# Second layer's tile of four experts: one expert's chunk to a ring tile, in rows of 4 KB instead of 2 KB

## The chip, the cores and the metric

The kernel runs on one core of one Trainium2 chip. The metric is the device time of one launch in microseconds (us); times of runs are given as the median of three.

## The reference

Two layers, each a mixer (three kinds of attention) and then a mixture of 16 experts. Only the experts of the second layer bear on this change. There the tokens are the 256 of the latent sequence, each routed to two experts:

```
def moe(tokens, router_w, router_b, w1, w3, w2):      # w1, w3: 16 x 1024 x 512; w2: 16 x 512 x 1024, f32
    ...
    gates = jnp.sum(jax.nn.one_hot(eidx, N_EXPERTS) * wsel[..., None], 1)
    def expert_step(acc, p):
        w1e, w3e, w2e, ge = p
        y = (jax.nn.silu(tokens @ w1e) * (tokens @ w3e)) @ w2e
        return acc + ge[:, None] * y, None
    out, _ = lax.scan(expert_step, jnp.zeros_like(tokens), (w1, w3, w2, gates.T))
```

The weights of one expert are three matrices of 2 MB, 6 MB in all, and each expert's are read once.

## The kernel before

**Expert weights.** The host lays out `wexp[layer, expert, chunk]` as six chunks of 1 MB for each expert, each of 128 rows (partitions) by 2048 f32 (8 KB a row). Chunks 0 and 1 are w1, 2 and 3 are w3, 4 and 5 are w2. A chunk of w1 or w3 holds four slices of the contraction (`kk`), 512 columns each; a chunk of w2 holds two slices of 1024 columns.

**Tiles of tokens.** The experts are ranked by their number of tokens, and `PLANS[1]` packs them on tiles of 128 token rows: seven tiles, `t` = 0 to 6. Tile 1 has four experts with 32 rows each (`_four(8, 9, 10, 11)`), the six others two experts each. For a tile TensorE runs `up(t)` (four chunks: w1, then w3, out to PSUM), `hidden(t)` (four transposes), `down(t)` (the two chunks of w2), and around these `dispatch` (gathers the tile's tokens, line 1828), `to_tokens` (lines 1635, 1619) and `combine` (lines 1850, 1851). In the trace the matmuls of `up` are line 1672 and those of `down` line 1771; each f32 matmul of the program is two instructions there. The order on TensorE is the code's: up(0), dispatch(1), hidden(0), down(0), up(1) with the combines of tile 0 between its chunks 2 and 3, dispatch(2), up(2) with hidden(1) after its first chunk, dispatch(3), down(1), up(3), dispatch(4), down(2), and so on.

**The stream of weights.** All weights of the kernel go through one list (`want`) in the order in which they are used, and are loaded by DMAs issued on SyncE's queue (line 194 for a load of several pieces, 198 for one). The buffers are ring tiles of 1 MB, 16 of them in this stage. `ws.take()` hands the next loaded ring tile to TensorE's code; `ws.done()` gives its buffer back, and the next load of the list is written for that buffer. A load into a buffer waits until the matmuls that read the tile before it are done. Each DMA on the queue also waits for the eighth DMA ahead of it to land, since eight completion semaphores (DMAHW0 to DMAHW7) are used in turn: at most eight are in flight. The ring tiles are numbered through the program; the names w194 to w277 below are the last 84. In the list, in this order:

- w182 to w193: the 12 MB of tile 0;
- w194 to w209: chunks 0 to 3 of tile 1 (four experts, 16 MB);
- w210 to w217: chunks 0 to 3 of tile 2 (two experts, 8 MB);
- w218 to w225: chunks 4 and 5 of tile 1 (8 MB);
- w226 to w277: tile 3's chunks 0 to 3, tile 2's chunks 4 and 5, and so on, all of two experts.

The numbers of the experts from w194 on are read from a register that the router sets (line 1485).

**How a ring tile is filled.** With two experts a ring tile holds one half (1024 columns) of each one's chunk: two DMAs of 512 KB, rows of 4 KB. With four experts it holds a quarter (512 columns) of each one's chunk: four DMAs of 256 KB, rows of 2 KB. One `ws.take()` of the four-expert tile therefore serves one slice `kk` in `up` (four groups of 32 rows, one for each expert) or half a slice in `down`, and is followed by its `ws.done()`.

Of the kernel before, what the change touches and what calls it, by code (L numbers as in the profile page):

```python
# [132 lines left out]
class Stream:  # L133
# [29 lines left out]
    def pump(self, most=None, after=None):  # L163

        end = min(len(self.aps), self.known) if most is None else min(len(self.aps), self.known, self.next + most)
        while self.next < end:
            n = self.next
            for r in reversed(self.rings):
                if r["free"] and n < r["limit"]:
                    r["free"] -= 1  # L170
                    break
            else:
                r = None
                if not self.rooms:
                    return
            if r is None:
                t = self.rooms.pop(0)
                parts = [t[:, 0:1024], t[:, 1024:2048]]
            elif r["halves"]:
                parts = [r["pool"].tile([128, 1024], F32R, tag=t, name=f"w{n}")[:].bitcast(F32) for t in r["tag"]]  # L180
            else:
                t = r["pool"].tile([128, 2048], F32, tag=r["tag"], name=f"w{n}", bufs=r["bufs"])
                parts = [t[:, 0:1024], t[:, 1024:2048]]
            if after is not None:
                self.nc.scalar.copy(parts[0][:, 0:1], after)
            src = self.aps[n]
            if isinstance(src, tuple):
                if len(src) == 4:
                    parts = [p[:, 512 * k:512 * k + 512] for p in parts for k in range(2)]
                for p, s in zip(parts, src):  # L190
                    src = s() if callable(s) else s
                    if len(src.shape) == 3:
                        p = p.rearrange("p (k f) -> p k f", k=src.shape[1])
                    load = self.nc.sync.dma_start(p, src)
                self.tiles[n] = parts
            else:
                self.tiles[n] = t[:, :self.widths[n]]
                load = self.nc.sync.dma_start(self.tiles[n], src() if callable(src) else src)
            self.load_of[n] = load.ins
            self.ring_of[n] = r  # L200
            self.next += 1
# [35 lines left out]
def build(tc, x_in, ctx_in, wada, win, wout, wexp, wqkv, rw, prm_in, bro_in, lnr, cst_in, out, dbg=None):  # L237
# [4 lines left out]
    G, T, S = nc.gpsimd, nc.tensor, nc.sync  # L242
# [49 lines left out]
    def want_exp(l):  # L292
        def by_columns(s, c, n):
            w = weights(l, s, c)

            def half():
                src = w() if callable(w) else w
                return src.rearrange("p (k f) -> p k f", k=2)[:, :, 512 * n:512 * n + 512]
            return half

        def part(t, lo, hi):
            ss = slots_of(l, t)
            if l and (t, lo) == (len(PLANS[l]) - 1, 4):

                for n in range(2):
                    for c in range(lo, hi):
                        want(tuple(by_columns(s, c, n) for s in ss), 2048)
                return
            for c in range(lo, hi):
                if len(ss) == 1:  # L310
                    want(weights(l, ss[0], c), 2048)
                else:
                    w = 2048 // len(ss)
                    for k in range(len(ss)):
                        want(tuple(weights(l, s, c, slice(w * k, w * k + w)) for s in ss), 2048)

        n = len(PLANS[l])
        part(0, 0, 4)
        for t in range(n):
            if t + 1 < n:  # L320
                if l and t == 0:
                    part(0, 4, 6)
                if slots_of(l, t + 1)[0] == 2:
                    marks["known", l] = len(aps)
                if l and t + 2 == n:

                    part(t, 4, 6)
                part(t + 1, 0, 4)
            if l == 0 or (t and t + 2 != n):
                part(t, 4, 6)  # L330
# [872 lines left out]
    for l in range(DEPTH):  # L1203
# [443 lines left out]
        def up(t, between):  # L1647

            o = sbig()
            x = xs_of.pop(t)  # L1650
            for c in range(4):
                if len(plan[t]) == 1:
                    xH, xL = x
                    if not first_splits:
                        raw = ws.take()
                    ob = o[:, halves[c // 2]]
                    early = len(first_splits) > 0
                    for q in range(2):
                        h, lo = first_splits.pop(0) if early else wsplit(raw[:, 1024 * q:1024 * q + 1024])
                        kk = 4 * (c % 2) + 2 * q  # L1660
                        mm6([(ob, xH[:, kk + k, :], xL[:, kk + k, :], h[:, halves[k]], lo[:, halves[k]]) for k in range(2)],
                            kk == 0, kk == 6, (0, 2, 1))
                    if not early:
                        ws.done()
                else:
                    nq = 4 // len(plan[t])
                    for c2 in range(len(plan[t])):
                        raw = ws.take()
                        for q in range(nq):
                            kk = 4 * (c % 2) + nq * c2 + q  # L1670
                            for r0, r1, e in groups(t):
                                T.matmul(o[r0:r1, halves[c // 2]], lhsT=x[:, kk, r0:r1], rhs=raw[e][:, halves[q]],  # L1672
                                         start=(kk == 0), stop=(kk == 7), skip_group_check=True)
                        ws.done()
                for s in between[c]:
                    s()
            u = ex.tile([128, 512], F32, tag="u", name="u", bufs=2)
            A.activation(u, o[:, 0:512], AF.Sigmoid)
            V.scalar_tensor_tensor(u, u, gms.pop(t), o[:, 0:512], op0=ALU.mult, op1=ALU.mult)
            V.tensor_mul(u, u, o[:, 512:1024])  # L1680
            us[t] = u
# [17 lines left out]
        def down(t, between=((),) * 4, final=None, pieces=None):  # L1699
# [63 lines left out]
            else:  # L1763
                o = sbig()
                four = len(plan[t]) == 4
                for kk in range(4):
                    for n in range(2):
                        if four or n == 0:
                            raw = ws.take()
                        for r0, r1, e in groups(t):  # L1770
                            T.matmul(o[r0:r1, halves[n]], lhsT=u[:, kk, r0:r1], rhs=raw[e][:, halves[0 if four else n]],  # L1771
                                     start=(kk == 0), stop=(kk == 3), skip_group_check=True)
                        if four or n:
                            ws.done()
                    for s in between[kk]:
                        s()
            for n in range(2):
# [534 lines left out]
```

## Time and profile before

| | us |
|---|---|
| median of three runs | 1265.35 |
| lowest and highest | 1263.18, 1268.04 |
| the profiled execution | 1269.78 |
| its span, first to last instruction | 1268.0 |

The profiled execution is one run more; the difference of 1.78 between its time and its span lies around the program. Rows below are from its trace, with times in us from the start of the span.

### The profile page before, as it was taken

The page shows a single profiled execution, that of the slowest core. Times are in us where ns is not written, and L with a number is a line of the kernel's source. Part 1 is how long each engine was busy: PE and PEld are TensorE (multiplying, and loading weights), DVE is VectorE, ACT ScalarE, POOL GpSimd, SP SyncE. Part 2 cuts the span into 40 slices and gives each one's busy share as a digit, 9 for nine tenths or more (in the row PEclk, how much of TensorE's full clock was granted, in tenths as well). Part 3 has the DMA queues.
Part 4 walks back from the last instruction along what each step waited for, and adds up shares of the span by engine and source line. Part 5 has one row for each costly group of instructions (what it writes and reads, how often), then busy time and mean ns, then how long its engine had stood idle before and what let it go on. Part 6 is the DMA issues. An engine that isn't in the chain of part 4 may idle for free. (4 is left out here: it accounts for less than half of the span.)

```text
span 1268.0 us, 18050 instructions
## 1 busy us (share of the span) xinstructions
PE 1141.0 (90%) x6433; PEld 745.0 (59%) x6433; DVE 664.2 (52%) x1340; ACT 472.5 (37%) x871; POOL 349.4 (28%) x344
## 2 busy tenths in 40 slices
PE   6999999998996898999989689999989699899984
PEld 4898764556785655555466478975547443334431
DVE  3545375626568965654478666546545812012133
ACT  4423456335235544434145364545343210101112
POOL 0242220231043634543464356221140100101001
PEclk9999999998996899999989889999999799999996
DMA  9543008661446889999995212502675899999992
GB/s 351 177 141 131 1 1 308 262 262 67 176 161 239 312 326 374 394 400 412 414 350 234 84 43 87 187 11 99 216 278 204 308 351 371 343 410 408 409 403 102
DMA packets 79213, 310.75 MB, mean 245 GB/s; under 512 B 9344, under 2 KB 10512, under 8 KB 64784
## 3 DMA queue, kind: packets, MB, share of 16 engines
q1 hardware_dynamic: 70864, 287.77, 59.7%
q10 hardware_dynamic: 5376, 13.40, 3.0%
q0 software_dynamic: 2880, 8.39, 2.3%
q8 instruction: 52, 0.85, 0.3%
q14 instruction: 41, 0.34, 0.1%
HBM read 304.74 MB, written 6.89 MB: 246 GB/s over the span
## 5 line engine op out<-in xcount | busy, mean ns | idle before, releaser
L232 DVE TENSOR_TENSOR wl<-w,wh 128x640 fp32r<-128x640 f32 (+3 forms) x133 | 162.8, 1242 | 52.1 <-ACT wh L232 50.7
L232 ACT CAST wh<-w 128x1024 fp32r<-128x1024 f32 (+2 forms) x135 | 132.7, 1006 | 105.2 <-PE s L447 34.7
L1245 POOL TENSOR_TENSOR wl<-w,wh 128x384 fp32r<-128x384 f32 x96 | 129.1, 1384 | 121.9 <-ACT wh L232 119.7
L1672 PE MATMUL s<-w,x 128*32 128x512 f32 (+1 forms) x640 | 111.5, 609 | 5.3 <-DMA w<-in_wexp_dram 5.3
L1771 PE MATMUL s<-w,uH 128*32 128x512 f32 (+1 forms) x480 | 81.9, 596 | 1.6 <-DMA w<-in_wexp_dram 0.9
L232 DVE TENSOR_REDUCE mxv<-s 128x2 f32<-128x1024 f32 (+1 forms) x54 | 56.3, 1044 | 48.7 <-PE s L1113 20.1
L232 ACT ACTIVATE P<-s,mxv 128x512 f32<-128x512 f32 (+1 forms) x108 | 65.9, 618 | 41.3 <-DVE mxv L232 22.5
L1672 PEld LDWEIGHTS s<-w,x 128*32 128x32 f32 (+1 forms) x640 | 30.6, 121 | 72.1 <-issue 52.1
L232 DVE TENSOR_TENSOR yL<-s,yH 128x512 fp32r<-128x512 f32 x22 | 15.1, 687 | 81.9 <-ACT yH L232 81.8
L445 PE MATMUL acc<-wh,hH 128*128 128x384 f32 (+3 forms) x148 | 52.5, 358 | 4.3 <-ACT hH L232 4.3
L232 ACT ACTIVATE u<-s 128x512 f32<-128x512 f32 x19 | 11.3, 596 | 120.6 <-PE s L1672 112.3
L446 PE MATMUL s<-wl,hH 128*128 128x384 f32 (+2 forms) x148 | 52.8, 357 | 3.0 <-DVE wl L232 3.0
L1819 POOL TENSOR_TENSOR xr<-xr,lr 128x1024 f32<-128x1024 f32 x4 | 9.4, 2360 | 161.4 <-ACT lr L232 161.4
L1672 PE MATMUL s<-w,xH 128*32 128x512 f32 (+1 forms) x352 | 53.6, 595 | 0.0
L445 PE MATMUL s<-wh,hH 128*128 128x384 f32 (+2 forms) x148 | 52.9, 357 | 0.0
L447 PE MATMUL s<-wh,hL 128*128 128x384 f32 (+2 forms) x148 | 52.7, 356 | 0.0
L1771 PEld LDWEIGHTS s<-w,uH 128*32 128x32 f32 (+1 forms) x480 | 22.3, 118 | 51.1 <-issue 36.2
L446 PE MATMUL acc<-wl,hH 128*128 128x384 f32 (+3 forms) x148 | 51.7, 349 | 0.0
L1643 PE MATMUL s<-wl,xH 128*128 128x512 f32 x128 | 44.2, 422 | 7.5 <-DVE wl L232 6.9
L447 PE MATMUL acc<-wh,hL 128*128 128x384 f32 (+3 forms) x148 | 50.7, 352 | 0.0
L514 PE MATMUL acc<-w,sc 128*32 128x512 f32 x320 | 45.7, 602 | 3.9 <-DMA w<-in_wada_dram 3.9
L232 DVE SCALAR_TENSOR_TENSOR u<-u,gp,s 128x512 f32<-128x512 f32 x19 | 14.1, 742 | 65.8 <-ACT u L232 65.8
(534 smaller groups left out, 2531.3 us busy)
## 6 DMA issues: line engine op xcount, KB each, us to landing
w<-in_wexp_dram SPq DMA_DIRECT2D x236, 512.0 KB
w<-in_wexp_dram SPq DMA_DIRECT2D x48, 1024.0 KB
w<-in_wada_dram SPq DMA_DIRECT2D x46, 1024.0 KB
w<-in_wexp_dram SPq DMA_DIRECT2D x96, 256.0 KB
w<-in_win_dram SPq DMA_DIRECT2D x8, 1024.0 KB
w<-in_wout_dram SPq DMA_DIRECT2D x8, 1024.0 KB
w<-in_win_dram SPq DMA_DIRECT2D x9, 768.0 KB
row<-rowd ACTq DMA_DIRECT2D x9, 512.0 KB
```

The costliest lines, as they stand in the source:

```text
L232: return f(*args, **kw)
L445: T.matmul(o, lhsT=lh, rhs=rh, start=start, stop=False, skip_group_check=True)
L446: T.matmul(o, lhsT=lh, rhs=rl, start=False, stop=False, skip_group_check=True)
L447: T.matmul(o, lhsT=ll, rhs=rh, start=False, stop=stop, skip_group_check=True)
L514: T.matmul(box["o"][32 * c:32 * c + 32, :], lhsT=sc32[:, k, :], rhs=w[:, 512 * c:512 * c + 512], start=(k == 0), stop=(k == 7), skip_group ...
L1245: last_split[0] = G.tensor_tensor(lo[:, c:], raw[:, c:], h[:, c:].bitcast(F32), op=ALU.subtract).ins
L1643: T.matmul(o, lhsT=ll if ps_ == 2 else lh, rhs=rl if ps_ == 1 else rh, start=start and j == 0 and not (same and n), stop=stop and j == 2 a ...
L1672: T.matmul(o[r0:r1, halves[c // 2]], lhsT=x[:, kk, r0:r1], rhs=raw[e][:, halves[q]], start=(kk == 0), stop=(kk == 7), skip_group_check=True)
L1771: T.matmul(o[r0:r1, halves[n]], lhsT=u[:, kk, r0:r1], rhs=raw[e][:, halves[0 if four else n]], start=(kk == 0), stop=(kk == 3), skip_group ...
L1819: G.tensor_tensor(x1[:, i, :], x1[:, i, :], lr, op=op)
```

## The change

In the stream, the loads of the four-expert tile are no longer cut by columns across experts: for each chunk there are four ring tiles, one for each expert, each holding that expert's whole chunk as two halves of 1024 columns. The branch that cut ring tiles into four pieces goes. In `up`, TensorE's code takes four ring tiles at once, runs the four slices of the chunk with the expert's own tile as the right-hand side, and gives the four back after the last slice; `down` takes four, runs two slices, and gives the four back. The arithmetic, the order of the matmuls and the number of ring tiles stay.

```
             if isinstance(src, tuple):
-                if len(src) == 4:
-                    parts = [p[:, 512 * k:512 * k + 512] for p in parts for k in range(2)]
                 for p, s in zip(parts, src):
...
-                    w = 2048 // len(ss)
-                    for k in range(len(ss)):
-                        want(tuple(weights(l, s, c, slice(w * k, w * k + w)) for s in ss), 2048)
+                    cols = [slice(1024 * k, 1024 * k + 1024) for k in range(2)]
+                    if len(ss) == 4:
+
+                        for s in ss:
+                            want(tuple(weights(l, s, c, k) for k in cols), 2048)
+                        continue
+                    for k in cols:
+                        want(tuple(weights(l, s, c, k) for s in ss), 2048)
...
-                    nq = 4 // len(plan[t])
-                    for c2 in range(len(plan[t])):
-                        raw = ws.take()
-                        for q in range(nq):
-                            kk = 4 * (c % 2) + nq * c2 + q
+                    four = len(plan[t]) == 4
+                    for c2 in range(1 if four else 2):
+                        raw = [ws.take() for _ in range(4 if four else 1)]
+                        for q in range(4 if four else 2):
+                            kk = 4 * (c % 2) + 2 * c2 + q
                             for r0, r1, e in groups(t):
-                                T.matmul(o[r0:r1, halves[c // 2]], lhsT=x[:, kk, r0:r1], rhs=raw[e][:, halves[q]],
+                                rhs = raw[e][q // 2][:, halves[q % 2]] if four else raw[0][e][:, halves[q]]
+                                T.matmul(o[r0:r1, halves[c // 2]], lhsT=x[:, kk, r0:r1], rhs=rhs,
                                          start=(kk == 0), stop=(kk == 7), skip_group_check=True)
-                        ws.done()
+                        for n in range(ws.used - len(raw), ws.used):
+                            ws.done(n)
...
                 for kk in range(4):
+                    if not four or kk % 2 == 0:
+                        raw = [ws.take() for _ in range(4 if four else 1)]
                     for n in range(2):
-                        if four or n == 0:
-                            raw = ws.take()
                         for r0, r1, e in groups(t):
-                            T.matmul(o[r0:r1, halves[n]], lhsT=u[:, kk, r0:r1], rhs=raw[e][:, halves[0 if four else n]],
+                            rhs = (raw[e][kk % 2] if four else raw[0][e])[:, halves[n]]
+                            T.matmul(o[r0:r1, halves[n]], lhsT=u[:, kk, r0:r1], rhs=rhs,
                                      start=(kk == 0), stop=(kk == 3), skip_group_check=True)
-                        if four or n:
-                            ws.done()
+                    if not four or kk % 2:
+                        for n in range(ws.used - len(raw), ws.used):
+                            ws.done(n)
```

On SyncE's queue, the first loads of the four-expert tile, right behind the reading of the experts' numbers (a DMA's row names the ring tile and its shape in f32; what it waits for stands in brackets; the rows between that set its address are left out). Before, one ring tile:

```order
L194 DMA w194_8680<-in_wexp_dram 128x512 [waits DMAHW3_49]
...
L194 DMA w194_8680<-in_wexp_dram 128x512 [waits DMAHW4_49]
...
L194 DMA w194_8680<-in_wexp_dram 128x512 [waits DMAHW5_49]
...
L194 DMA w194_8680<-in_wexp_dram 128x512 [waits DMAHW6_49]
...
L194 DMA w195_8685<-in_wexp_dram 128x512 [waits DMAHW7_49]
```

And now two ring tiles, and the first that waits for a buffer:

```order
L192 DMA w194_8680<-in_wexp_dram 128x1024 [waits DMAHW3_49]
...
L192 DMA w194_8680<-in_wexp_dram 128x1024 [waits DMAHW4_49]
...
L192 DMA w195_8683<-in_wexp_dram 128x1024 [waits DMAHW5_49]
...
L192 DMA w195_8683<-in_wexp_dram 128x1024 [waits DMAHW6_49]
...
L192 DMA w198_8772<-in_wexp_dram 128x1024 [waits DMAHW3_49,PE_49]
```

A ring tile is two DMAs of twice the size, the tile's 96 DMAs become 48, and the eight in flight are 4 MB where they were 2 MB.

On TensorE, the start of `down(1)` (w218 and w219 are ring tiles, uH the hidden values; a row with x4 is one matmul for each of the four experts). Before:

```order
L1771 MATMUL s_9323<-w218_9057,uH_9204 32x512 x4
L1771 MATMUL s_9323<-w219_9066,uH_9204 32x512 x4
L1771 MATMUL s_9323<-w220_9075,uH_9204 32x512 x2
L1771 MATMUL s_9323<-w220_9076,uH_9204 32x512 x2
L1771 MATMUL s_9323<-w221_9085,uH_9204 32x512 x2
L1771 MATMUL s_9323<-w221_9086,uH_9204 32x512 x2
```

And now, where a row is one expert's matmul:

```order
L1777 MATMUL s_9275<-w218_9037,uH_9156 32x512
L1777 MATMUL s_9275<-w219_9040,uH_9156 32x512
L1777 MATMUL s_9275<-w220_9043,uH_9156 32x512
L1777 MATMUL s_9275<-w221_9047,uH_9156 32x512
...
L1777 MATMUL s_9275<-w222_9083,uH_9156 32x512
L1777 MATMUL s_9275<-w223_9087,uH_9156 32x512
```

The first matmuls read one ring tile before; now the first four read four of them, and none of the four is given back before the sixteenth.

## Rows read from the trace of the kernel before

**Rows 1.** The page: the span in 40 equal slices of 31.7 us.

```profile
DMA  9543008661446889999995212502675899999992
GB/s 351 177 141 131 1 1 308 262 262 67 176 161 239 312 326 374 394 400 412 414 350 234 84 43 87 187 11 99 216 278 204 308 351 371 343 410 408 409 403 102
```

**Rows 2.** The page: DMA issues, count and KB of each.

```profile
w<-in_wexp_dram SPq DMA_DIRECT2D x236, 512.0 KB
...
w<-in_wexp_dram SPq DMA_DIRECT2D x96, 256.0 KB
```

**Rows 3.** Windows: stretch, busy time of engines, granted clock, DMA share, GB/s.

```profile
1000.00:1009.00 9.00, 4.99 (x30) 5.02 (x31) 8.83 (x42) 0.59 (x1) 0.00 (x0) 0.59 0.70 236
1009.00:1060.00 51.00, 49.85 (x299) 20.05 (x299) 11.71 (x36) 5.35 (x10) 0.00 (x0) 1.00 1.01 341
1061.00:1080.00 19.00, 17.73 (x154) 7.66 (x154) 2.75 (x8) 2.71 (x5) 0.00 (x0) 1.00 1.03 410
1081.00:1106.00 25.00, 24.08 (x127) 9.41 (x128) 1.44 (x2) 2.97 (x5) 4.68 (x2) 1.00 0.99 331
1110.00:1230.00 120.00, 115.69 (x684) 48.24 (x678) 24.50 (x48) 15.03 (x27) 4.68 (x2) 0.99 1.03 408
...
1240.00:1250.00 10.00, 9.04 (x34) 2.56 (x30) 2.78 (x5) 0.62 (x1) 0.00 (x0) 0.86 0.18 71
```

**Rows 4.** Windows at the edges of these stretches, and from 1110 to 1115.

```profile
1060.00:1061.00 1.00, 1.00 (x3) 0.16 (x3) 0.00 (x0) 0.02 (x1) 0.00 (x0) 1.00 0.99 369
1080.00:1081.00 1.00, 0.34 (x7) 0.02 (x3) 0.00 (x0) 0.00 (x0) 0.00 (x0) 1.00 1.02 365
1107.00:1108.00 1.00, 0.00 (x1) 0.00 (x0) 0.28 (x1) 0.59 (x1) 0.00 (x0) 1.00 1.00 385
1110.00:1115.00 5.00, 5.00 (x36) 1.62 (x32) 0.00 (x0) 0.04 (x1) 0.00 (x0) 0.68 1.03 409
```

**Rows 5.** Waits of SyncE's queue, 960 to 1245: us in total, times, longest.

```profile
SPq L194 <- DMA w<-in_wexp_dram: 105.8, 158, 2.2
...
SPq L194 <- PE s L1672: 3.9, 11, 0.6
SPq L194 <- PE s L1771: 2.2, 8, 0.4
```

**Rows 6.** Timeline of TensorE around up(1): start, us, instructions, idle before.

```profile
1037.80 7.07 PE L1672 MATMUL s<-w,x 128*32 128x512 f32 x64
...
1045.52 3.64 PE L1672 MATMUL s<-w,x 128*32 128x512 f32 x32
...
1051.87 7.52 PE L1672 MATMUL s<-w,x 128*32 128x512 f32 x30
1059.90 1.04 PE L1672 MATMUL s<-w,x 128*32 128x512 f32 x2 [0.51 <-DMA w<-in_wexp_dram]
1060.87 3.84 PE L1828 MATMUL tp<-O,h2a 128*128 128x128 f32 x32
1064.64 1.92 PE L1672 MATMUL s<-w,x 128*32 128x512 f32 x16
```

**Rows 7.** Timeline of TensorE around down(1) and the start of up(3).

```profile
1088.58 6.85 PE L1771 MATMUL s<-w,uH 128*32 128x512 f32 x36
...
1099.90 7.11 PE L1771 MATMUL s<-w,uH 128*32 128x512 f32 x20 [0.16 <-DMA w<-in_wexp_dram]
1109.00 5.34 PE L1672 MATMUL s<-w,x 128*32 128x512 f32 x32 [1.99 <-DMA w<-in_wexp_dram]
```

**Rows 8.** Waits of TensorE's weight loads, 1037 to 1110.

```profile
PEld s L1771 <- DMA w<-in_wexp_dram: 12.4, 19, 1.5
PEld s L1672 <- DMA w<-in_wexp_dram: 12.1, 15, 1.6
```

**Rows 9.** Waits of TensorE's weight loads, 1110 to 1250.

```profile
PEld s L1672 <- DMA w<-in_wexp_dram: 6.8, 9, 1.5
...
PEld s L1771 <- DMA w<-in_wexp_dram: 0.3, 1, 0.3
```

## The prediction

> **What bounds the kernel now.** I read the page's slices first [rows 1]. The DMA digits say 9 in two late places; the last begins a little before slice 32 (32 x 31.7 = 1014 us) and holds until slice 38, so from the start of the second layer's experts the DMA engines are never idle. Busy is not fast, though: under the same 9s the line in GB/s says 351, 371, 343 and then 410. The page's list of DMAs shows what differs: 96 loads of 256 KB, the four-expert tile's and nothing else's, beside the 512 KB loads of the two-expert tiles [rows 2].
>
> The windows put the two side by side in the order of the stream [rows 3]. While w194 to w209 arrive (four experts, rows of 2 KB) the DMAs are busy 1.01 and move 341 GB/s; while w210 to w217 arrive (two experts, 4 KB) they move 410; w218 to w225 (four experts again) 331; everything behind, 408. The share of busy time is 0.99 to 1.03 in all four, so the engines are not kept waiting: they take longer for the same bytes. The windows at the edges [rows 4] read 369 at 1060, 365 at 1080 and 385 at 1107, each between the two levels, so the rate changes with the kind of load and not with what TensorE does.
>
> Is the stream what the end waits for? SyncE's queue waited 105.8 us in this stage for an older DMA to land (its eight in flight) and only 3.9 + 2.2 us for matmuls to free a buffer [rows 5]: the stream holds itself up, TensorE doesn't hold it. TensorE in turn waits for the stream, in `up(1)`, `up(2)`, `down(1)`: its weight loads waited 12.1 + 12.4 us for w from 1037 to 1110 [rows 8], and `up(3)` starts at 1109.00 on the landing of w226 [rows 7]. From 1110 on the waits are 6.8 + 0.3 us [rows 9], and the stream runs at 408 until it ends near 1242 (a share of 0.18 in the 10 us from 1240) [rows 3]: the two keep the same pace, and both start this last part from one event, the landing of w226 at 1109.0. What moves that event moves the end.
>
> **The change, part by part.**
>
> *The loads.* 96 DMAs of 256 KB become 48 of 512 KB: 16 + 8 ring tiles of 1.049 MB, 25.2 MB, the same bytes. Their form becomes that of the two-expert tiles' loads, 128 rows of 4 KB, which have their rate in the trace: 410 GB/s, so 2.557 us for a ring tile. Two ways to get the gain:
> - By landing times. By the windows' sum, w192 and w193, 2.1 MB, are all there is before w194: 9.0 us at 236 GB/s [rows 3] is 2.1 MB, so w194 begins near 1009.0. The edges [rows 4] put w209's end at 1060.4, w217's at 1080.9 and w225's at 1106.4. The 16 tiles took 51.4 us and would take 16 x 2.557 = 40.9, a gain of 10.5. The 8 took 25.5 and would take 20.5, a gain of 5.0. Sum 15.5.
> - By rates: 51.4 x (1 - 341/410) = 8.6 and 25.5 x (1 - 331/410) = 4.9. Sum 13.5. The two differ because the windows hold some bytes that are not the tile's.
>
> I take the middle, 14.5 us earlier for w226 (1094.5).
>
> SyncE's own work falls by 48 issues; since it mostly waits, that is worth nothing. The eight in flight become 4 MB; the two-expert tiles have had that all along.
>
> *TensorE in groups of four ring tiles.* Count and shape of the matmuls stay. What moves is the landing that the first of a group waits for, and the release.
> - `up(1)`: its first two chunks start at 1037.80 without a wait [rows 6]. Its fourth chunk (w206 to w209) starts at 1051.87 and now takes 7.52 + 1.04 us to 1060.9, where the third, unhindered, takes 3.64 [rows 6]. By the new times w209 lands at 1009.0 + 40.9 = 1049.9, or 1051.8 by rates: before its chunk starts. So the chunk ends at 1055.5, 5.4 us earlier.
> - From there 3.8 us of dispatch(2), then `up(2)`, the gains' row and dispatch(3), which took from 1064.64 to 1088.58 [rows 6, 7], 23.9 us with some 2 to 3 us of waits in it: `down(1)` starts near 1081 instead of 1088.58.
> - `down(1)` is two groups. The second (w222 to w225) cannot finish before w225 lands, near 1091.5, and the products that then remain are at most one slice's eight matmuls in the program (16 of the trace, half of a chunk's 3.64 us, so 1.8). The first chunk of `up(3)` takes 5.34 us [rows 7] against 3.64: after TensorE's rest the granted clock is 0.68 of 2.4 GHz on the mean there, part of it at 1.2 [rows 4]. That stays.
> - `up(3)` waits for w226, which lands 2.6 us behind w225, later than these 1.8 us. The grouping is covered by that landing; without that cover it would cost up to 1.8.
>
> *The buffers.* Tile w210 needs the buffer of w194, which was free after one slice; now it is free after the chunk, at 1037.8 + 7.07/2 = 1041.3. The new stream would want to issue it when w206's first half lands, 1009.0 + 12.5 x 2.557 = 1041.0. Seven DMAs are then in flight, 7 x 1.28 = 9 us of work, so a release that is 0.3 us late costs nothing. The later ones have more: w214 wants the buffer of w198 at 1051.2, which is free at 1044.9.
>
> *Behind w226* nothing changes: same loads, same work. The waits of 7.1 us that TensorE has there [rows 9] go with the stream. DVE, ScalarE and GpSimd keep their rows.
>
> **The sum.** 1268.0 - 14.5 = 1253.5 for the span, 1255.3 for an execution like the profiled one (1269.78). That one lies 4.4 above the median of the three runs, 1265.35; a stage paced by the same loads should be alike in them, so the median goes to 1265.35 - 14.5 = 1250.9, rounded to 1251.
>
> **A rule that speaks against it.** The Trainium skill, page "DMA: Bandwidth & Descriptors", section "Specifications", says that a transfer needs 512 B or more for the line's full rate. By that rule 2 KB rows have it already, and the sum would be nought: 1265. The trace differs, with 341 and 331 GB/s against 410 in neighbouring stretches of one stage.
>
> **The rivals.**
> - *No gain: the rate belongs to something that stays* (that four experts are read at a time, the stretch's own traffic), not to the form of the loads. For it: form, number of experts and size of a DMA change together, so the trace doesn't part them. Against: the rate falls twice, 60 us apart, with the form both times. Time 1265, chance 6 in 100, the page's rule within it.
> - *TensorE takes over part of it.* If the second group of `down(1)` meets the lower clock after a longer rest, at the pace of 5.34 for 3.64, and runs wholly behind w225, `up(3)` starts up to 5.3 - 2.6 = 2.7 us late, and its own first chunk loses 1.7 more; or loads in pairs from one expert run at a rate between 341 and 410. Gain 7 to 11: 1254.5 to 1258.5. For it: from 1110 on TensorE waits little, so what it loses there is not all given back. Chance 15 in 100.
> - *Slower: the stream runs dry at the releases.* Four buffers come back at once. If a group's last product came over 9 us after the moment at which the next loads want its buffers, the engines would stop, and each further us is lost: six groups, each at most its 10.2 us of loading. Against it: the latest release, w194's, is 0.3 us behind. The earliest loss needs TensorE 9 us later at 1037.8 than its row; with the gain of 14.5 to be outweighed, two groups must run dry for over 7 us and 14 together pass 1272. Chance 3 in 100, 1272 or more.
> - The forecast, 12 to 17 us gained (1248 to 1253.5): chance 76 in 100.
>
> **How the numbers follow.** The bounds of the gain are 13.5 and 15.5, and the medians of such runs differ by two or three (1263.18 to 1268.04 here). The range, 1246 to 1259, holds the forecast and the part-gain. About 0.5% (6.3 us) is what a measurement can tell from no change. Faster by more: forecast and part-gain, 0.91. Same: 0.06. Slower: 0.03.
>
> **What would show it.** The trace after should have no loads of 256 KB; some 410 GB/s from 1010 without a step, where 341 and 331 stood; `up(1)`'s last chunk in 3.6 us without a wait; `up(3)`'s start near 1094.5; SyncE's wait for matmuls still a few us. A stretch below 400 GB/s with the DMAs busy shows the first rival right; DMAs idle before 1090, with SyncE waiting for line 1676 or 1777, the third; TensorE still in `down(1)` when w226 has landed, the second.

## The result and the profile after

| | before | after |
|---|---|---|
| median, us (four runs each, beside one another) | 1266.69 | 1252.16 |
| lowest and highest | 1263.18, 1268.96 | 1250.54, 1258.09 |
| the profiled execution, its span | 1269.78, 1268.0 | 1250.54, 1248.8 |

The ratio of the times is 0.9896, with a 95% interval of 0.9855 to 0.9937: 14.5 us faster, at 1252.2 where 1251.0 was forecast.

The page of the kernel after, slices of the span and the DMA issues (KB of each, median us from issue to landing), beside [rows 1, 2]:

```profile
DMA  9543008761445999999997112420763899999992
GB/s 354 181 143 133 1 1 303 272 270 68 150 188 211 333 336 375 389 402 411 413 348 295 51 52 81 151 84 4 300 252 131 331 402 409 408 409 408 409 402 96
...
w<-in_wexp_dram SPq DMA_DIRECT2D x284, 512.0 KB, 10.2
```

There are no loads of 256 KB any more, and the late 9s stand over 402 to 409 GB/s throughout. The windows of the kernel after, cut where the stages lie (columns as in [rows 3]):

```profile
1005.00:1044.00 39.00, 38.76 (x254) 16.83 (x251) 7.38 (x25) 4.76 (x9) 0.00 (x0) 1.00 1.03 409
1045.00:1065.00 20.00, 19.86 (x170) 9.11 (x174) 4.64 (x11) 2.73 (x5) 0.00 (x0) 1.00 1.03 408
1066.00:1085.00 19.00, 15.42 (x118) 7.88 (x110) 1.43 (x2) 2.96 (x5) 4.69 (x2) 1.00 1.02 409
1090.00:1095.00 5.00, 4.33 (x40) 1.24 (x36) 1.38 (x2) 0.95 (x3) 0.00 (x0) 1.00 1.02 407
1095.00:1205.00 110.00, 105.37 (x632) 45.46 (x634) 23.39 (x46) 14.85 (x27) 4.68 (x2) 1.00 1.03 408
```

The steps from 341 to 410 and down to 331 are gone: the last column hardly moves. The timeline of TensorE after, for the chunks of [rows 6, 7]:

```profile
1003.80 7.09 PE L1676 MATMUL s<-w,x 128*64 128x512 f32 x32
...
1039.97 3.64 PE L1676 MATMUL s<-w,x 128*32 128x512 f32 x32
...
1046.32 3.64 PE L1676 MATMUL s<-w,x 128*32 128x512 f32 x32
1049.89 3.84 PE L1835 MATMUL tp<-O,h2a 128*128 128x128 f32 x32
...
1074.85 4.48 PE L1777 MATMUL s<-w,uH 128*32 128x512 f32 x34
1080.78 1.04 PE L1777 MATMUL s<-w,uH 128*32 128x512 f32 x2 [1.45 <-DMA w<-in_wexp_dram]
1083.34 1.04 PE L1777 MATMUL s<-w,uH 128*32 128x512 f32 x2 [1.51 <-DMA w<-in_wexp_dram]
1085.90 3.62 PE L1777 MATMUL s<-w,uH 128*32 128x512 f32 x26 [1.51 <-DMA w<-in_wexp_dram]
1089.83 1.92 PE L1676 MATMUL s<-w,x 128*32 128x512 f32 x16 [0.31 <-DMA w<-in_wexp_dram]
1092.29 1.92 PE L1676 MATMUL s<-w,x 128*32 128x512 f32 x16 [0.53 <-DMA w<-in_wexp_dram]
```

And the same stage's start, `up(0)`, in the timeline of the kernel before:

```profile
1009.35 7.09 PE L1672 MATMUL s<-w,x 128*64 128x512 f32 x32
```

`up(3)` starts at 1089.83 instead of 1109.00, 19.2 us earlier, but 5.55 of these lie ahead of `up(0)` (1003.80 against 1009.35), where nothing was changed: over the kernels below that start lies anywhere from 1002 to 1013. So the stage is measured from here on from the start of `up(0)` to the start of `up(3)`: 99.65 us before, 86.03 after, a gain of 13.6. From the start of `up(3)` to the end of the span there are 159.0 us in both. The waits after, of SyncE's queue (940 to 1245) and of TensorE's weight loads (1030 to 1090), beside [rows 5, 8]:

```profile
SPq L192 <- DMA w<-in_wexp_dram: 125.5, 167, 2.2
```

```profile
PEld s L1777 <- DMA w<-in_wexp_dram: 8.7, 7, 2.4
...
PEld s L1676 <- DMA w<-in_wexp_dram: 1.6, 5, 0.4
```

The waits of TensorE fell from 24.5 to 10.3 us, and the stream still holds itself up.

### The profile page after: what moved, and what is told of

The parts are those of the page before. It is cut to its first block, busy times and chain, and to the rows that moved or that the text cites. A ratio compares the mean times of both kernels' runs of the same rounds, so it can differ in the third digit from the quotient of the medians.

```text
span 1248.8 us, 17900 instructions
## 1 busy us (share of the span) xinstructions
PE 1125.1 (90%) x6433; PEld 741.9 (59%) x6433; DVE 663.4 (53%) x1340; ACT 472.3 (38%) x871; POOL 348.1 (28%) x344
## 5 line engine op out<-in xcount | busy, mean ns | idle before, releaser
L1676 PE MATMUL s<-w,x 128*32 128x512 f32 (+1 forms) x640 | 104.5, 596 | 2.2 <-DMA w<-in_wexp_dram 2.1
L1777 PE MATMUL s<-w,uH 128*32 128x512 f32 (+1 forms) x480 | 74.6, 595 | 5.2 <-DMA w<-in_wexp_dram 4.5
L1646 PE MATMUL s<-wh,xH 128*128 128x512 f32 x128 | 43.9, 426 | 2.3 <-ACT wh L230 2.3
```

Of the source, the lines that this page charges most:

```text
L1646: T.matmul(o, lhsT=ll if ps_ == 2 else lh, rhs=rl if ps_ == 1 else rh, start=start and j == 0 and not (same and n), stop=stop and j == 2 a ...
L1777: T.matmul(o[r0:r1, halves[n]], lhsT=u[:, kk, r0:r1], rhs=rhs, start=(kk == 0), stop=(kk == 3), skip_group_check=True)
```

## The experiments

The time came, then, from the stream's rate in the two stretches of the four-expert tile. But the change gives its loads four things at once: rows of 4 KB for 2 KB, loads of 512 KB for 256, 4 MB in flight for 2, and experts read one after the other, where before the four were read in turn at the same columns. My theory was the first, a price for each row. The rivals were the other three, and TensorE's groups. A fifth that no expectation names is SyncE's own work: half the loads are half the issues. The table lists all runs: GB/s in the first and second stretch, "stage" from `up(0)` to `up(3)` in the profiled execution, and the ratio to the kernel before beside it on the chip. A stage is one execution, so a microsecond in it is not much; where stage and time disagree, both are given.

| | rows | load | in flight | read | GB/s | stage, us | ratio, 95% |
|---|---|---|---|---|---|---|---|
| before | 2 KB | 256 KB | 2 MB | four in turn | 341, 331 | 99.65 | |
| e4 | 2 KB | 256 KB | 2 MB | four in turn | 342, 337 | 99.0 | 0.9964 to 1.0013 |
| e7 | 2 KB | 256 KB | 2 MB | two in turn | 339, 318 | 100.5 | 0.9936 to 0.9997 |
| e6 | 2 KB | 256 KB | 2 MB | four in turn, other columns | 377, 363 | 91.6 | 0.9929 to 0.9971 |
| e3 | 2 KB | 256 KB | 2 MB | one by one | 375, 360 | 92.8 | 0.9902 to 0.9960 |
| e10 | 4 KB | 256 KB | 2 MB | one by one | 359, 350 | 95.5 | 0.9961 to 1.0006 |
| e11 | 4 KB | 512 KB | 2 MB | one by one | 356, 328 | 93.9 | 0.9957 to 0.9996 |
| e9 | 1 KB | 512 KB | some 3 MB | one by one | 349, 348 | 95.9 | 0.9966 to 1.0007 |
| e1 | 2 KB | 512 KB | 4 MB | one by one | 388, 387 | 90.5 | 0.9895 to 0.9944 |
| e12 | 2 KB | 512 KB | 4 MB | four in turn | 387, 386 | 90.0 | 0.9901 to 0.9950 |
| after | 4 KB | 512 KB | 4 MB | one by one | 409, 409 | 86.03 | 0.9855 to 0.9937 |
| e8 (after again) | 4 KB | 512 KB | 4 MB | one by one | 409, 410 | 86.7 | 0.9862 to 0.9912 |
| e2 | 4 KB | 256 KB | 2 MB | by halves of the partitions | 248, 241 | 129.5 | 1.0191 to 1.0295 |
| e5 | up as after, down as before | | | | 410, 334 | 91.2 | 0.9918 to 0.9958 |

**First set: row length, load size, order, groups.**

e1: the changed kernel, whose 512 KB loads take every other 2 KB of a row.

```diff
-                            want(tuple(weights(l, s, c, k) for k in cols), 2048)
+                            want(tuple(by_columns(s, c, n) for n in range(2)), 2048)
```

> As the changed kernel, but each of the two 512 KB loads of a ring tile reads every other 2 KB piece of the chunk's rows, so that its rows are of 2 KB again; number and size of the loads, the eight in flight (4 MB) and TensorE's groups stay. If the length of a row alone sets the rate (the step as the prediction took it), the two stretches run at 331 to 341 GB/s again and the whole gain is lost: 1264 to 1268 us, up(3) some 14 us later behind the start of up(0) than in the changed kernel. If the size of a load or the bytes in flight set it, the rate is that of the last tile's loads, which have this very form (512 KB in rows of 2 KB) and moved 388 to 391 GB/s before as after: 25.2 MB take 64.7 us against 61.4 at 410, so 3 us of the gain are lost: 1255. If four experts side by side in a ring tile were the trouble, it stays at 1252 to 1255.

It gave 1256.79 against 1267.53. The windows of e1:

```profile
1010.00:1048.00 38.00, 37.36 (x247) 16.56 (x244) 7.60 (x21) 4.76 (x9) 0.00 (x0) 1.00 1.05 388
1071.00:1091.00 20.00, 14.58 (x102) 7.18 (x102) 1.44 (x2) 2.96 (x5) 4.67 (x2) 0.99 1.05 387
```

With the rows as short as before, 10.7 us of the gain stay (9.2 in the stage). Short rows cost 409 to 388 GB/s, but not down to 341.

e2: the rows stay 4 KB, each load is cut into two of 64 neighbouring partitions.

```diff
+                to = parts if len(src) == 2 else [p[64 * r:64 * r + 64] for p in parts for r in range(2)]
...
-                            want(tuple(weights(l, s, c, k) for k in cols), 2048)
+                            want(tuple(of_rows(s, c, k, r) for k in cols for r in range(2)), 2048)
```

> As the changed kernel, but each 512 KB load is cut in two by partitions (rows 0 to 63, 64 to 127): 256 KB each, rows of 4 KB, eight in flight are 2 MB, 96 loads again. If the length of a row alone sets the rate: 408 to 410 GB/s, 1252 us as the changed kernel. If the size of a load or the bytes in flight set it: 336 to 360 GB/s in the two stretches, 25.2 MB in 70 to 75 us, so 9 to 14 us of the gain are lost: 1261 to 1266. If four experts side by side were the trouble: 1252.

It gave 1296.1 against 1267.53, slower by 28.6. The window of e2:

```profile
1010.00:1073.00 63.00, 48.00 (x258) 18.20 (x254) 9.07 (x23) 4.76 (x9) 0.00 (x0) 0.90 1.04 248
```

None of the theories had this. Loads to 64 neighbouring partitions were a new disturbance, so the run says nothing on the size of loads; e10 repeats it with other partitions.

e3: one expert to a ring tile as in the change, but loaded in four quarters of 256 KB, rows of 2 KB.

```diff
-                            want(tuple(weights(l, s, c, k) for k in cols), 2048)
+                            want(tuple(weights(l, s, c, slice(512 * q, 512 * q + 512)) for q in range(4)), 2048)
```

> One expert's chunk to a ring tile and TensorE's groups as in the changed kernel, but loaded in four pieces of 256 KB with rows of 2 KB, the form of load of the kernel before. Row length or size of a load: 331 to 341 GB/s, 1264 to 1268 us, no gain. Four experts side by side in a ring tile: 400 to 410 GB/s, 1252.

It gave 1257.22 against 1267.53. The first window of e3:

```profile
1010.00:1053.00 43.00, 42.36 (x285) 18.99 (x282) 9.43 (x24) 5.36 (x10) 0.00 (x0) 1.00 1.04 375
```

Rows, loads and bytes in flight have the size of before, and yet 10.3 us are gained by the medians, 6.9 of 13.6 in the stage: these sizes, even together, are not the whole cause. What differs from before is the order of reading, and TensorE's groups, which e4 tries alone.

e4: the loads of before, with TensorE's groups of four ring tiles.

```diff
+                    if four:
+                        raws = [ws.take() for _ in range(4)]
+                        for kk in range(4):
+                            for r0, r1, e in groups(t):
...
+                        for n in range(ws.used - 4, ws.used):
+                            ws.done(n)
```

> The kernel before with its loads as they are, but TensorE takes four ring tiles at a time and gives the four back after the last of their matmuls. By every theory of the loads the two stretches stay at 331 to 341 GB/s. The prediction has the groups covered by the landing of the next tile: within 2 us of the kernel before (1265 to 1268). If giving back four at once starves the stream, SyncE waits more than 10 us for matmuls in the stage and the time is 1272 or more.

It gave 1265.19 against 1267.53, no change. The windows of e4:

```profile
1007.00:1055.00 48.00, 46.58 (x284) 18.74 (x280) 9.06 (x23) 4.76 (x9) 0.00 (x0) 1.00 1.02 342
1077.00:1101.00 24.00, 22.56 (x116) 8.89 (x112) 1.44 (x2) 3.12 (x6) 4.68 (x2) 1.00 0.98 337
```

The groups cost and give nothing.

**Second set: the order of reading, and half of the change.**

e5: chunks 0 to 3 as in the change, 4 and 5 as before.

```diff
+                    if len(ss) == 4 and c > 3:
+                        for k in range(4):
+                            want(tuple(weights(l, s, c, slice(512 * k, 512 * k + 512)) for s in ss), 2048)
+                        continue
```

> Chunks 0 to 3 of the four-expert tile (w194 to w209) loaded as in the changed kernel, chunks 4 and 5 (w218 to w225) as before. The gain of the first stretch alone by the prediction: 8.6 to 10.5 us, so 1257; the second stretch stays near 331 GB/s. If TensorE could not turn the first stretch's gain into an earlier end (it waits mostly in down(1)), the gain would be under 4: 1263 or more.

It gave 1258.53 against 1267.08, 8.5 of the 15.5 us that the whole change gave beside it (e8). The rate changes at the seam, in the windows of e5:

```profile
1008.00:1044.00 36.00, 35.76 (x228) 15.90 (x228) 5.98 (x20) 5.16 (x10) 0.00 (x0) 1.00 1.03 410
1067.00:1095.00 28.00, 27.06 (x171) 10.33 (x162) 1.68 (x3) 2.96 (x5) 4.68 (x2) 1.00 1.00 334
```

e6: e4 with one change, that the four loads of a ring tile read four different quarters of the columns.

```diff
-                        want(tuple(weights(l, s, c, slice(w * k, w * k + w)) for s in ss), 2048)
+                        at = [w * ((k + i) % 4 if len(ss) == 4 else k) for i in range(len(ss))]
+                        want(tuple(weights(l, s, c, slice(a, a + w)) for s, a in zip(ss, at)), 2048)
```

> Four experts side by side in a ring tile, 256 KB loads with rows of 2 KB and TensorE in groups of four, all as in e4_groups_only; but the four loads of a ring tile read four different quarters of the experts' rows (expert i the quarter k + i modulo 4) instead of the same quarter. If the loss against e3_rows2k_256_one (some 375 GB/s where the kernel before has 331 to 341) comes from reading the same 2 KB of every 8 KB row in all the loads in flight, the rate goes to about 375 and the time to 1257. If it comes from four experts being read in turn, the rate stays at 331 to 345 and the time at 1264 to 1268.

It gave 1261.42 against 1267.08. The first window of e6:

```profile
1015.00:1058.00 43.00, 42.35 (x276) 18.60 (x276) 9.07 (x23) 4.76 (x9) 0.00 (x0) 1.00 1.04 377
```

The same bytes in loads of the same form, only in another order, go 10% faster than in e4. The rate came as expected, the time did not: 5.7 us gained where 10 were expected, though the stage is 8.1 us shorter.

e7: two experts to a ring tile, their loads in turn at the same quarter.

```diff
+                        for two in (ss[:2], ss[2:]):
+                            for k in range(2):
+                                want(tuple(weights(l, s, c, slice(512 * q, 512 * q + 512))
+                                           for q in (2 * k, 2 * k + 1) for s in two), 2048)
```

> Two experts side by side in a ring tile, each with half a chunk in two loads of 256 KB and rows of 2 KB, issued in turn (first, second, first, second expert); the eight in flight touch two experts, as in e3_rows2k_256_one, where the experts come one after the other. If the number of experts in flight sets the loss: about 375 GB/s, 1257 us. If it is the change of expert from load to load: 331 to 350, 1262 to 1267. If it is the same quarter of the rows in all loads in flight: about 375, since the eight hold all four quarters.

It gave 1264.15 against 1267.08. The windows of e7:

```profile
1013.00:1060.00 47.00, 45.58 (x282) 18.26 (x278) 9.07 (x23) 4.76 (x9) 0.00 (x0) 1.00 1.00 339
1082.00:1106.00 24.00, 18.57 (x132) 8.34 (x124) 1.43 (x2) 2.97 (x5) 4.69 (x2) 1.00 0.97 318
```

By these rates two loads in a row at the same quarter are as bad as four. The reading is weaker than the others: the profiled execution, 1270.39 us, is the longest of e7's ten, and by the times e7 and e6 are not parted (their intervals overlap).

e8: the changed kernel once more, beside these.

> The changed kernel once more, beside the kernels above and on their chip: 1252 us, 408 to 410 GB/s in both stretches, so that the differences to it are taken within one set of runs.

It gave 1251.56 against 1267.08, 15.5 us faster.

**Third set: bytes in flight against the price of a row.** So far the order accounts for 341 to 375, but not for e1's 388 or the 409. All kernels at 377 or less had 2 MB in flight.

e9: the 512 KB loads of the change take every other 1 KB.

```diff
+        def by_eighths(s, c, n):
+            return lambda: weights(l, s, c)().rearrange("p (k f) -> p k f", k=4)[:, :, 256 * n:256 * n + 256]
...
-                            want(tuple(weights(l, s, c, k) for k in cols), 2048)
+                            want(tuple(by_eighths(s, c, n) for n in range(2)), 2048)
```

> As e1_rows2k_512, but the 512 KB loads read every other 1 KB of the chunk's rows, rows of 1 KB; the columns lie in the ring tile in another order than the matmuls take them, so the products of these four experts are not the reference's. 2 KB rows gave 386 to 387 GB/s and 4 KB rows 408 to 410. If each row has a fixed price (4 KB at 410 GB/s is 160 ns on one of the 16 engines, 2 KB at 387 is 85 ns, so 5 us a thousand rows for each engine), a 1 KB row takes 47 ns and the rate is 350 GB/s: 25.2 MB in 71.9 us, 1263. If length of rows matters only beside same-quarter reads, it stays at 387: 1256.

It gave 1263.92 against 1265.95. The expected 350 came true, but the price of rows in the expectation is miscounted: with one of 16 engines at 84.7 ns for a row of 2 KB (387 GB/s) and 160.2 for 4 KB (409), an engine's price for a row is 2 x 84.7 - 160.2, some 9 ns and not 5. A price of 9 ns would also give the 47.0 ns for a row of 1 KB (16 x 1024 B / 348.5 GB/s), but e9 does not show it, since it has another thing that differs. SyncE's issues in e9 from 1008 to 1050 (ns: shortest, median, longest; then us to landing):

```profile
L192 SPq DMA_DIRECT2D w<-in_wexp_dram x30: 333/1215/1678, 1007.2 to 1049.8; - x30
...
DMA to landing us min/median/max: 8.6/8.8/9.5
```

An issue takes 1.2 us, and SyncE never waits for a landing in this stretch. At 349 GB/s and 8.8 us some 3 MB are in flight, not 4. Whether the engines hold SyncE up (the DMA share, 1.10, is the highest of all) or SyncE them is not parted.

e10: e2 with every other partition in a load in place of 64 neighbours.

```diff
-                to = parts if len(src) == 2 else [p[64 * r:64 * r + 64] for p in parts for r in range(2)]
+                to = parts if len(src) == 2 else [p[r::2] for p in parts for r in range(2)]
```

> As e2_rows4k_256 (256 KB loads with rows of 4 KB), but each load takes every other partition instead of 64 neighbours. If the 245 GB/s of e2 came from 64 neighbouring partitions as the target, this brings the rate back: near 400 if small loads cost little (e3 against e1: 376 to 387 in the first stretch), 1253 to 1255. If it came from the number of partitions in a load or from its size, 245 GB/s stays: 1290 or more.

It gave 1262.71 against 1265.95, with 359 and 350 GB/s; its interval, 0.9961 to 1.0006, does not tell it from no gain. Rows of 4 KB did not bring the rate here, but SyncE is in the way, as its issues and its waits from 1005 to 1050 show:

```profile
L193 SPq DMA_DIRECT2D w<-in_wexp_dram x64: 332/475/1137, 1004.8 to 1049.0; - x64
```

```profile
SPq L193 <- DMA w<-in_wexp_dram: 0.2, 1, 0.2
```

A load of 64 partitions takes it 475 ns to issue, where one of 128 partitions by 4 KB takes 333, and in 45 us it waits 0.2 us for a landing: its issuing paces the stream. So e10 gives no price for load size or bytes in flight; e11 leaves SyncE's issues as in the change.

e11: the changed kernel, where each load of the tile also waits for the fourth ahead of it to land, so that 2 MB are in flight.

```diff
+                    if n in self.behind:
+                        if len(self.recent) >= 4:
+                            self.tc.add_manual_dep(load.ins, self.recent[-4].name, mybir.DependencyInfo(
+                                mybir.DependencyClass.Sync, mybir.DependencyReason.DATA))
+                        self.recent.append(load.ins)
```

> The changed kernel, but each load of the four-expert tile also waits for the fourth load ahead of it: 512 KB loads with rows of 4 KB, four in flight, 2 MB as before the change. If the bytes in flight make up what load size and reading order do (256 KB loads: e7 and the kernel before 331 to 345 GB/s, e10 some 360, all with 2 MB in flight), the two stretches fall to 340 to 375 GB/s, unevenly from window to window: 1257 to 1263. If the size of a load itself matters, or the order of the reads, they stay at 400 to 410: 1252.

It gave 1262.81 against 1265.82. The windows of e11, the first stretch and three pieces of it:

```profile
1011.00:1053.00 42.00, 39.86 (x262) 17.26 (x262) 9.07 (x23) 4.75 (x9) 0.00 (x0) 1.00 0.97 356
1015.00:1020.00 5.00, 5.00 (x25) 1.73 (x26) 1.19 (x6) 0.09 (x1) 0.00 (x0) 1.00 0.96 359
1020.00:1025.00 5.00, 5.00 (x37) 3.46 (x34) 1.43 (x2) 1.18 (x2) 0.00 (x0) 1.00 0.94 301
1025.00:1030.00 5.00, 4.76 (x32) 2.89 (x32) 0.00 (x0) 1.66 (x3) 0.00 (x0) 1.00 0.98 375
```

The very loads of the change, and 409 is gone: the rate is 301 to 375 in neighbouring pieces, while the DMA share reads 0.94 to 0.98. In the second stretch it is 328, under the 340 expected. SyncE is not what holds it: of the 89 us from 1008 to 1097 it waits 55.1 for a landing:

```profile
SPq L193 <- DMA w<-in_wexp_dram: 55.1, 57, 5.0
```

The theory that row length sets the rate fell here and in e1.

e12: 4 MB in flight with the rest against it: rows of 2 KB, and the four experts read in turn at the same columns (two quarters to a load, where the loads of before have one).

```diff
-                        for s in ss:
-                            want(tuple(weights(l, s, c, k) for k in cols), 2048)
+                        for n in range(2):
+                            for two in (ss[:2], ss[2:]):
+                                want(tuple(by_columns(s, c, n) for s in two), 2048)
```

> As e1_rows2k_512 (512 KB loads, rows of 2 KB), but the four experts are read in turn, each time the same two quarters, two experts to a ring tile: the order of the kernel before with loads of twice the size. If reading the same quarter in turn costs by itself (e7 against e3, the kernel before against e6), the rate falls from 387 to about 350: 1262. If it costs only in 256 KB loads, with 2 MB in flight, 386 to 388 GB/s stay, as in the last tile's loads: 1256.

It gave 1254.42 against 1265.82. The windows of e12, cut alike:

```profile
1007.00:1043.00 36.00, 35.73 (x238) 15.80 (x234) 6.97 (x20) 4.76 (x9) 0.00 (x0) 1.00 1.05 387
1015.00:1020.00 5.00, 5.00 (x38) 3.62 (x35) 1.43 (x2) 1.18 (x2) 0.00 (x0) 1.00 1.05 384
1020.00:1025.00 5.00, 4.76 (x31) 2.69 (x31) 0.00 (x0) 1.66 (x3) 0.00 (x0) 1.00 1.05 386
1025.00:1030.00 5.00, 5.00 (x27) 1.91 (x24) 0.00 (x0) 0.49 (x1) 0.00 (x0) 1.00 1.05 387
```

A steady rate, the same as e1's: with 4 MB in flight this order of reading costs nothing.

**The account.** e11 and the changed kernel issue the same loads and differ only in how many may be in flight: 356 and 328 GB/s against 409 and 409, 93.9 us of stage against 86.0, a gain of 3.0 us in time against 14.5. So what is in flight is shown as a cause, worth 7.9 us of stage, with row length, load size and the number of issues left alone; whether it is the bytes or the number of loads, e11 does not part. Between before and e12 the bytes in flight double, with the loads' size and with half the issues, while rows stay and the order nearly does: 99.65 to 90.0 us, 9.6 of the stage's 13.6. From e12 to after the rows double: 90.0 to 86.0, 4.0 (the order changes as well, which e1 against e12 shows to be worth nothing here). By rates it is the same: 16 ring tiles of 1.049 MB at 341, 387 and 409 GB/s and 8 at 331, 386 and 410 take 74.5, 65.1 and 61.5 us, so 9.4 and 3.6. The shares hang on the way taken: by e3 and e1 the new order comes first, with 6.9 us, then the bytes in flight with 2.3, then the rows with 4.5. Order and bytes in flight remove one and the same loss in part; only the rows have much the same price on both ways. That larger loads help by the bytes in flight alone is argued and not shown: no run has 256 KB loads with 4 MB in flight.

SyncE's issuing is closer to a limit with 256 KB loads than the totals of [rows 5] say. Its waits for a landing from the first stretch to the end of the second, 98 us before (1009 to 1107) and 87 after (1003 to 1090):

```profile
SPq L194 <- DMA w<-in_wexp_dram: 28.9, 57, 1.4
```

```profile
SPq L192 <- DMA w<-in_wexp_dram: 49.9, 67, 1.1
```

It does not hold the rate at 341, since e3 and e6 issue as many loads of that form and reach 375 and 377; what it costs at these rates is not shown. Why 2 MB in flight do not keep the rate, and why reading the same columns in turn then costs 375 to 341, stays open: no run here looks behind the DMA engines' queues. e11's 356, with longer rows than e3's 375, is open too. No kernel tried beats the changed one.

## Why the prediction was right, and where a step was not

- **What bounds the kernel, and the sum.** Right. The stream's rate set the landing of w226, and that the end: 14.5 us were forecast, 14.5 and 15.5 (e8) measured, with 13.6 in the stage, at the lower end of the step's 13.5 to 15.5. Its way by landing times, 15.5, was too large: at 341 GB/s the 16 ring tiles take 49.2 us, not the 51.4 read off the edges. That the first median met the middle of the two is partly luck. The half done alone gave 8.5, where the sum had 8.6 to 10.5 for the first stretch.
- **"So the engines are not kept waiting: they take longer for the same bytes."** The engines did take longer: share divided by rate, a byte took 9% more of them before (1.01 at 341) than in e12 (1.05 at 387). But e12 has the rows of before, so the step from there to the form of the loads failed; the total did not show it, since the loads of the two-expert tiles have 410 by either reading. A DMA share near 1 does not tell what a stream could do: it is 1.02 at 342 GB/s (e4), 0.94 at 301 (e11), 1.05 at 387 (e12), 1.03 at 409. "The eight in flight become 4 MB" stood in the prediction without a price; it was 7.9 of the 13.6 us by e11 and, with the loads' size, 9.6 by e12 (2.3 where the order is already that of the change, e3 against e1). A reader of the step would have taken e11's loads for the gain, and they give 3 us.
- **"Since it mostly waits, that is worth nothing."** This of SyncE's 48 issues read [rows 5] over 285 us; over the two stretches of the kernel before SyncE waited 28.9 us of 98 for a landing, so it did not mostly wait. What the fewer issues gave is not parted, but e11, which has them, falls to 356 and 328 GB/s, so they alone do not give the rate.
- **A row that was overlooked.** The last tile's loads in the kernel before are 512 KB in rows of 2 KB, cut by columns. The window of the kernel before there:

```profile
1230.00:1232.00 2.00, 2.00 (x12) 0.85 (x10) 2.00 (x5) 0.00 (x0) 0.00 (x0) 1.00 1.06 391
```

  391 GB/s, not 341: it parts the length of rows from the rest, and shows that rows alone cost some 4 to 5% (391 here and 388 in e1, against 408 to 409).
- **The Trainium skill's rule.** The prediction set the Trainium skill's line of 512 B ("DMA: Bandwidth & Descriptors", "Specifications") against the trace. With 4 MB in flight rows of 2 and 4 KB, both above that line, run at 387 and 409 GB/s, so the runs differ from the rule; but most of 341 to 410, which the prediction held against it, was no matter of rows.
- **`up(1)` and `down(1)`.** Right. The fourth chunk takes 3.64 us without a wait and, counted from `up(0)`, ends 5.4 us earlier (1046.32 + 3.64 + 5.55 = 1055.5 against 1060.9), as forecast. `down(1)` starts at 1074.85, which is 1080.4 on the old scale; 1081 was said.
- **The cover of `down(1)`'s second group.** Right in sign, wrong in size. "At most one slice's eight matmuls", 1.8 us, was said to remain behind w225. In the timeline after, 26 instructions, 3.62 us, stand behind the last wait: the first round of a slice now reads four ring tiles, so TensorE waits for w223, w224 and w225 in turn and does nearly all of the group behind them. That wait is for the first half of w225; the second half (512 KB, some 1.3 us at 409 GB/s) leaves some 2.3 us, an estimate. The cover by w226 was 0.31 us, not 0.8. In e8 it was gone, and the rival in which TensorE takes a part had begun; the next point has the rows.
- **The lower clock in `up(3)`.** "That stays" did not hold in this execution: the granted clock is 1.00 from 1090 to 1095, at 2.4 GHz, where it was 0.68 [rows 4], and 16 instructions take 1.92 us. It was worth nothing, since TensorE waits 0.53 us for the next ring tile at 1092.29 in any case. But in e8, the same kernel, the clock fell earlier, in `down(1)`: 0.50 from 1086 to 1091, at 1.2 GHz.

```profile
1086.00:1091.00 5.00, 4.51 (x24) 1.19 (x28) 0.00 (x0) 0.00 (x0) 0.00 (x0) 0.50 1.02 406
```

```profile
1081.37 1.04 PE L1777 MATMUL s<-w,uH 128*32 128x512 f32 x2 [0.98 <-DMA w<-in_wexp_dram]
1083.93 1.04 PE L1777 MATMUL s<-w,uH 128*32 128x512 f32 x2 [1.51 <-DMA w<-in_wexp_dram]
1086.49 6.14 PE L1777 MATMUL s<-w,uH 128*32 128x512 f32 x25 [1.51 <-DMA w<-in_wexp_dram]
1091.61 1.02 PE L1676 MATMUL s<-w,x 128*32 128x512 f32 x3
```

  There 25 instructions take 6.14 us and `up(3)` starts without a wait, 0.7 us later behind `up(0)` than in the other execution. TensorE had waited three times just before in both, so no row shows why the clock fell in one alone. The end did not move by it: from the start of `up(0)` to the end of the span there are 245.0 us in the first and 244.0 in e8.
- **Releases.** The stream's waits for matmuls of these lines fell from 6.1 to 1.9 us, none over 0.3, in the waits of SyncE's queue after:

```profile
SPq L192 <- PE s L1676: 1.0, 5, 0.3
SPq L192 <- PE s L1777: 0.9, 3, 0.3
```

  The stream never ran dry: the rival on the slow side had nothing.

## What to carry to other kernels

When a queue admits a fixed number of transfers, a smaller load also means fewer bytes in flight, and more issues for the engine that issues them. Look at the rate over pieces of a few microseconds and at the issuing engine's waits, and not at the DMA's busy share: at shares near 1 the pieces moved between 301 and 375 GB/s in e11 and between 384 and 387 in e12. Before a gain is put down to one property of a load, look for another stretch of the same trace that has this property alone. The order in which loads walk through memory can be worth as much as their form, as long as few bytes are in flight.

## What the runs showed of the hardware

- Loads of 64 neighbouring partitions move 248 and 241 GB/s (e2); loads of the same size with every other partition 359 and 350 (e10), where SyncE's issuing paces them. The Trainium skill, page "SBUF — State Buffer", section "Door 1: The DMA port swizzle (why `[64,N]` ≈ `[32,N]`)", maps partitions 0 to 63 to eight of 16 ports. This agrees in direction; half of its 435 GB/s, an estimate of 218, lies below the 248 measured. That the ports are the cause is not shown: e10 reads other rows too.
- With eight loads of 512 KB in flight, rows of 2 KB run at 387 GB/s and rows of 4 KB at 409 (e1, e12, after): some 9 ns for a row on its engine, an estimate from these two.
- An issue takes SyncE 333 ns for 128 rows of 2 or 4 KB (before, after), 543 for 256 rows of 2 KB (e1, e12), 475 for 64 rows of 4 KB in every other partition (e10), and 1215 for 512 rows of 1 KB (e9); these are medians in the first stretch.
- The changed kernel's loads move 409 GB/s with eight in flight and 356 and 328 with four (e11).
- With 2 MB in flight, reading the same quarter of the columns of expert after expert costs 375 to 341 GB/s (e3, e6 against e4, e7); with 4 MB, nothing (e12 against e1).
